# A hybrid encoder layer on one core: six passes per token half at both ends of the up phase, splits at the joint on VectorE, and the down projection's last part as a plain product

## The chip, the cores and the metric

The kernel runs on one core of one Trainium2 chip. The metric is the device time of one execution in microseconds, given as the median of several runs. One further execution was recorded by the hardware profiler; all rows of the trace come from it.

## The reference, cut to what matters

One layer of an encoder is applied with the same weights to two groups of tokens, 1024 and 256 of them, 1280 in all. The mixing part (a bidirectional gated DeltaNet and a grouped-query attention, side by side) is not touched by the change. What follows it is:

```
D_MODEL = 1024
D_FF = 4 * D_MODEL
...
    mix = jnp.concatenate([o_a, o_b], axis=-1) @ w_out
    x = x + _rmsnorm(mix, norm_mix_post)
    hm = _rmsnorm(x, norm_mlp_pre)
    f = jnp.square(jax.nn.relu(hm @ w_up)) @ w_down
    return x + _rmsnorm(f, norm_mlp_post)
```

## The kernel before

Every large product is done to nearly float32 accuracy by splitting each operand into a high half, rounded to a short format, and a low half, the rest: `split` (L77 to L80) casts on ScalarE (L79) and subtracts on VectorE or, where `leng=G` is given, on GpSimd (L80). A product is then three matmuls: high by high, low by high, high by low. G is GpSimd (POOL in the profile), V VectorE (DVE), S ScalarE (ACT), T TensorE (PE), SP the engine that issues the transfers.

**Out-projection.** A loop over ten tiles of 128 tokens (L1065 to L1091). For tile t it prepares the operands of tile t + 1 (`out_prep`), loads the rows of x (`x_tile`), issues 48 matmuls (`out_mm`), and does the two norms of tile t - 1 (`out_norm`): two large VectorE operations (L1010, L1015), each behind a chain of one-column operations. `to_M` then transposes the normed tile on TensorE (L1030) and writes four quarter blocks and three of their sums into the seven operands "mc"; two of these sums are on GpSimd. The last three tiles' `to_M` is put off into the up phase.

**Up phase.** hm @ w_up is done by Strassen-Winograd: for each 256 columns of w_up (a pass; 16 of them) and each half of the tokens (640), seven products of 12 matmuls 128x320 (`up_mm`). The seven activation operands are split once for each token half (`prep_m`, tiles mh and ml); the four sums of weight blocks are made for each pass (`up_sums`, tile us, GpSimd), and each of the seven weight operands is split for its product (`up_w`, tiles uhi and ulo). After a product VectorE adds it up from PSUM, ScalarE does relu and square, and GpSimd makes four sums s of the result (`up_post`) that the down phase needs; all seven results go to DRAM (r_d). The list PASSES orders this: the first NF = 3 passes run for token half 0 alone (single passes), since half 1 is not ready, the next 13 for both halves (double passes), and the last three for half 1 alone. Around it the loop over s, one step for each product of a pass, places by hand what else is issued: the norm and `to_M` of the last tiles in steps 0 to 4, the splits of half 1 in steps 8 to 20, alternating between GpSimd and VectorE, and from 21 steps before the end the first loads and splits of the down phase (`down_load`, with four weight sums on GpSimd; `down_r`; `down_prep`).

**Down phase.** The same algorithm over the other dimension, in eight parts of 512 rows of w_down. A part has seven steps; a step splits a row operand (fr into fhi and flo) and a weight operand (dw into dhi and dl), and `prod` does five tiles of six matmuls 128x512 and adds each from PSUM into one or two of the accumulators (ten tiles of 1024 columns).

**Last part.** The eighth part has its operands split ahead (`last_ops`, during part seven) and is done tile by tile, so that a tile is ready before the next. The two token halves of a tile need two corrections among the accumulators (`fix`, GpSimd), squares with sums on ScalarE whose unused output is a PSUM tile named junk (L1400), and the last norm (`rest`): one-column operations, a multiplication by the gain (GpSimd, L1411), the addition of x (L1423) and the write (L1425).

Instructions on one engine run in the order in which a scheduler placed them, so an instruction that waits holds all behind it.

## Time and profile before

| | |
|---|---|
| runs | 1779.65, 1782.5, 1783.88 us; median 1782.5 |
| the profiled execution's own time | 1782.71 us |
| its span | 1780.9 us |
| TensorE busy | 1634.0 us (92%), 9769 matmuls |
| VectorE busy | 1262.1 us (71%) |
| ScalarE busy | 849.0 us (48%) |
| GpSimd busy | 845.1 us (47%) |

A row of a timeline has the start in the span, the duration, engine, line and operation, then the tile written and the tiles read with their shape, and in brackets the idle time before it and what ended that. A row of a group has the line, engine, operation, tiles and count, then the busy sum in us, the mean of one in ns, and the idle time before them with those who ended it. A duration includes some pipelining: the next instruction of an engine can start before the end that is shown.

### The profile page before, as it was taken

Reading aid. Unit: us, or ns where it says so; the run is one execution under the profiler, and the core shown is the slowest. Engines: PE = TensorE matmul, PEld = TensorE weight load, DVE = VectorE, ACT = ScalarE, POOL = GpSimd, SP = SyncE. Lnnn points to the kernel's source line nnn. Section 1 sums busy time; section 2 is a strip of 40 time slices with the busy share of each in tenths; the row PEclk is TensorE's granted clock in tenths of the full one; section 3 lists DMA queues with packets and bytes.
Section 4 is the critical chain, followed back from the end, with each engine's and each line's share of the span. In section 5 each row is a group of like instructions: output and inputs, shape, how many; then the busy total and the mean of one; then the engine's idle time right before and its main releaser. Section 6 shows DMA issues by size and latency. Waiting matters only on the chain. (4 is left out here: it accounts for less than half of the span.)

```text
span 1780.9 us, 27898 instructions
## 1 busy us (share of the span) xinstructions
PE 1634.0 (92%) x9769; PEld 1395.0 (78%) x9769; DVE 1262.1 (71%) x2475; ACT 849.0 (48%) x1917; POOL 845.1 (47%) x709
## 2 busy tenths in 40 slices
PE   6999889889988999899887999999979999999984
PEld 5777777767767887578777999999978888888863
DVE  7546798996746878876667544544467878878988
ACT  5236567544336766764345454544545233333422
POOL 3212331321213344420349555445587777777855
PEclk9999999999989999999998999999989999999997
DMA  6113335455358765334323444343555444444125
GB/s 206 66 44 108 105 102 146 110 161 147 111 154 275 251 200 181 129 107 152 116 76 97 143 151 144 128 138 120 184 179 185 152 138 151 151 137 146 59 106 177
DMA packets 205516, 250.85 MB, mean 141 GB/s; under 512 B 35009, under 2 KB 159743, under 8 KB 205375
## 3 DMA queue, kind: packets, MB, share of 16 engines
q1 hardware_dynamic: 205231, 248.93, 44.1%
q8 instruction: 77, 1.26, 0.3%
q14 instruction: 64, 0.52, 0.1%
q0 software_dynamic: 144, 0.13, 0.0%
HBM read 158.57 MB, written 90.44 MB: 140 GB/s over the span
## 5 line engine op out<-in xcount | busy, mean ns | idle before, releaser
L1138 PE MATMUL pd<-mh,ulo 128*128 128x320 f32 x892 | 282.7, 317 | 19.8 <-DVE ulo L80 19.6
L1137 PE MATMUL pd<-mh,uhi 128*128 128x320 f32 x892 | 280.6, 315 | 8.4 <-ACT uhi L79 7.6
L1139 PE MATMUL pd<-ml,uhi 128*128 128x320 f32 x892 | 280.1, 314 | 0.0
L1279 DVE TENSOR_TENSOR acc<-acc,pd 128x512 f32<-128x512 f32 x380 | 238.3, 678 | 44.7 <-PE pd L1275 44.5
L1274 PE MATMUL pd<-dl,fhi 128*128 128x512 f32 x490 | 192.4, 393 | 0.0
L1273 PE MATMUL pd<-dhi,fhi 128*128 128x512 f32 x490 | 192.3, 393 | 0.0
L1275 PE MATMUL pd<-dhi,flo 128*128 128x512 f32 x490 | 191.8, 391 | 0.0
L1138 PEld LDWEIGHTS pd<-mh,ulo 128*128 128x128 f32 x892 | 172.1, 193 | 24.0 <-DVE ulo L80 24.0
L1137 PEld LDWEIGHTS pd<-mh,uhi 128*128 128x128 f32 x892 | 172.1, 193 | 10.1 <-ACT uhi L79 9.0
L369 PE MATMUL pt<-h_hi,wlo 128*128 128x512 f32 (+1 forms) x480 | 179.1, 373 | 0.0
L367 PE MATMUL pt<-h_hi,whi 128*128 128x512 f32 (+1 forms) x480 | 179.0, 373 | 0.0
L368 PE MATMUL pt<-h_lo,whi 128*128 128x512 f32 (+1 forms) x480 | 178.5, 372 | 0.0
L1139 PEld LDWEIGHTS pd<-ml,uhi 128*128 128x128 f32 x892 | 172.0, 193 | 0.0
L1255 ACT CAST fhi<-fr 128x1280 fp32r<-128x1280 f32 x49 | 62.1, 1267 | 218.2 <-PE pd L1274 120.0
L80 POOL TENSOR_TENSOR dl<-dw,dhi 128x1024 fp32r<-128x1024 f32 x49 | 130.6, 2666 | 39.6 <-ACT dhi L79 39.0
L727 POOL TENSOR_TENSOR P<-P,sm 128x512 f32<-128x512 f32 (+1 forms) x72 | 73.5, 1040 | 95.2 <-DVE sm L725 41.1
L80 DVE TENSOR_TENSOR ulo<-us,uhi 128x512 fp32r<-128x512 f32 x76 | 72.1, 951 | 52.6 <-ACT uhi L79 51.2
L1275 PEld LDWEIGHTS pd<-dhi,flo 128*128 128x128 f32 x490 | 91.9, 188 | 21.0
L1273 PEld LDWEIGHTS pd<-dhi,fhi 128*128 128x128 f32 x490 | 92.0, 188 | 20.9
L1274 PEld LDWEIGHTS pd<-dl,fhi 128*128 128x128 f32 x490 | 92.0, 188 | 20.4
L367 PEld LDWEIGHTS pt<-h_hi,whi 128*128 128x128 f32 x480 | 93.0, 194 | 13.4
L369 PEld LDWEIGHTS pt<-h_hi,wlo 128*128 128x128 f32 x480 | 92.9, 193 | 12.9
(353 smaller groups left out, 4087.7 us busy)
## 6 DMA issues: line engine op xcount, KB each, us to landing
fr<-r_d SPq DMA_DIRECT2D x49, 640.0 KB, 4.1
vis<-vis_d SPq DMA_DIRECT2D x64, 384.0 KB, 4.1
r_d<-s SPq DMA_DIRECT2D x128, 160.0 KB, 1.8
uraw<-in_w_up SPq DMA_DIRECT2D x19, 1024.0 KB, 5.3
dw<-in_w_down SPq DMA_DIRECT2D x32, 512.0 KB, 4.4
r_d<-u SPq DMA_DIRECT2D x96, 160.0 KB, 2.5
wraw<-in_w_in SPq DMA_DIRECT2D x48, 256.0 KB, 3.7
x<-in_x_prompt SPq DMA_DIRECT2D x16, 512.0 KB, 5.3
```

The costliest lines, as they stand in the source:

```text
L80: (V if leng is None else leng).tensor_tensor(lo, src, f32(hi), ALU.subtract)
L367: T.matmul(pm[:, :n], lhsT=whi, rhs=h_hi[:, k, t0:t0 + n], start=(k == 0), stop=False)
L368: T.matmul(pm[:, :n], lhsT=whi, rhs=h_lo[:, k, t0:t0 + n], start=False, stop=False)
L369: T.matmul(pm[:, :n], lhsT=wlo, rhs=h_hi[:, k, t0:t0 + n], start=False, stop=(k == KD - 1))
L727: G.tensor_tensor(x[:, :kw], x[:, :kw], sm[:, 0:1].to_broadcast([128, kw]), ALU.mult)
L1137: T.matmul(pm, lhsT=w[0][:, k], rhs=mh[b, i][:, k], start=(k == 0), stop=False)
L1138: T.matmul(pm, lhsT=w[1][:, k], rhs=mh[b, i][:, k], start=False, stop=False)
L1139: T.matmul(pm, lhsT=w[0][:, k], rhs=ml[b, i][:, k], start=False, stop=(k == 3))
L1273: T.matmul(pm, lhsT=r[0][:, k, tk], rhs=w[0][:, k], start=(k == 0), stop=False)
L1274: T.matmul(pm, lhsT=r[0][:, k, tk], rhs=w[1][:, k], start=False, stop=False)
L1275: T.matmul(pm, lhsT=r[1][:, k, tk], rhs=w[0][:, k], start=False, stop=(k == Q - 1))
L1279: V.tensor_tensor(half(t, d), half(t, d), pm, ALU.add)
```

## The change

Three things are changed together.

Single passes: NF goes from 3 to 6, so six passes run for token half 0 alone at the start of the up phase, ten for both halves, and six for half 1 alone at the end. The up phase has the same products in all.

The joint: of the seven operands of half 0, six instead of five are split before the up phase and the seventh in step 0. All these splits, those of half 1 (now in steps 10, 14, up to 34) and the two late sums of `to_M` for the last three tiles go to VectorE. In single passes `up_sums` is on VectorE as well, in double passes it stays on GpSimd. x has one buffer instead of two, and the load of tile t is issued behind the norm of tile t - 1. The norm of the last tile is put into steps 3 to 6, its `to_M` into step 7. At the end of the up phase the loads and splits of the down phase are spread over 42 steps, the weights ahead of the rows.

The last part: a plain product of 512 rows by 1024 columns, with four row blocks (one of them, a21, is now written to DRAM for the first two passes) and four weight blocks as they are loaded. Each token half of a tile and each half of its columns is one group of 12 matmuls, with one addition into its accumulator: 240 matmuls and 20 additions instead of 210 and 50. The weights' low halves are made on GpSimd during part seven, which has no sums of weights for a part eight any more. The corrections are issued a tile ahead, the squares' unused output is an SBUF tile, and the last norm is done for each token half by itself, the multiplications in two pieces of 512 columns.

The next rows show what that does to the order on three engines. TensorE in the out-projection: xt is the transposition of a normed tile, pmx the matmuls of the next tile; the piece of the difference stands near tile 7.

```order
@@ -3236,5 +3236,4 @@
 L916 MATMUL pmx<-wo_lo_9195,o_hi 128x512
 L917 MATMUL pmx<-wo_hi_9194,o_lo 128x512
-L1030 MATMUL xt<-ident,mix 128x128 x8
 L897 MATMUL otr<-ident,og 128x128 x4
 L915 MATMUL pmx<-wo_hi_9153,o_hi 128x512
@@ -3257,4 +3256,5 @@
 L917 MATMUL pmx<-wo_hi_9186,o_lo 128x512
 L915 MATMUL pmx<-wo_hi_9190,o_hi 128x512
+L1029 MATMUL xt<-ident,mix 128x128 x8
 L916 MATMUL pmx<-wo_lo_9191,o_hi 128x512
 L917 MATMUL pmx<-wo_hi_9190,o_lo 128x512
@@ -3286,7 +3286,7 @@
```

The transpositions of one tile stand further back, among the matmuls of the tile after. VectorE at the start of the up phase, before: ss and rsq belong to the last norm, mc to `to_M`, ulo to the weights' splits.

```order
L1008 TENSOR_TENSOR ss<-ss 128x1
L1040 TENSOR_TENSOR mc<-xt,mc 128x4x64
L987 TENSOR_SCALAR rsq<-ss 128x1
L80 TENSOR_TENSOR ulo<-uraw,uhi 128x512
L1041 TENSOR_TENSOR mc<-mc,xt 128x4x64
L1040 TENSOR_TENSOR mc<-xt,mc 128x4x128
L80 TENSOR_TENSOR ulo<-us,uhi 128x512
L1163 TENSOR_TENSOR u_10312<-u,pd 128x320
L80 TENSOR_TENSOR ulo<-us,uhi 128x512
```

And in the changed kernel, where us are the sums of weight blocks and ml is a split of an activation operand:

```order
L1007 TENSOR_TENSOR ss<-ss 128x1
L1039 TENSOR_TENSOR mc<-xt,mc 128x4x64
L1040 TENSOR_TENSOR mc<-mc,xt 128x4x64
L1041 TENSOR_TENSOR mc<-mc 128x4x64
L1128 TENSOR_TENSOR us<-uraw 128x512
L1042 TENSOR_TENSOR mc<-mc 128x4x64
L1129 TENSOR_TENSOR us<-us,uraw 128x512
L1130 TENSOR_TENSOR us<-uraw 128x512
L1131 TENSOR_TENSOR us<-uraw,us 128x512
L80 TENSOR_TENSOR ulo<-uraw,uhi 128x512
L80 TENSOR_TENSOR ulo<-us,uhi 128x512
L80 TENSOR_TENSOR ml<-mc,mh 128x1280
```

Sums that were on GpSimd and a split stand in VectorE's queue between the first weights' splits, and the late `to_M` stands ahead of them. VectorE in the last part, before: tile by tile, the additions of products (L1279) mixed with the results (L1423) of the tile before.

```order
L1279 TENSOR_TENSOR acc_15140<-acc_15140,pd 128x512
L1279 TENSOR_TENSOR acc_15135<-acc_15135,pd 128x512
L1423 SCALAR_TENSOR_TENSOR acc_15133<-acc_15133,rsq,x_17851 128x1024
L1279 TENSOR_TENSOR acc_15140<-acc_15140,pd 128x512
L1279 TENSOR_TENSOR acc_15135<-acc_15135,pd 128x512
L1279 TENSOR_TENSOR acc_15140<-acc_15140,pd 128x512 x2
L1279 TENSOR_TENSOR acc_15135<-acc_15135,pd 128x512 x2
L1423 SCALAR_TENSOR_TENSOR acc_15138<-acc_15138,rsq,x_17851 128x1024
L1279 TENSOR_TENSOR acc_15140<-acc_15140,pd 128x512 x2
```

And in the changed kernel, acc_15252 being token half 0 of the first tile and acc_15257 its half 1:

```order
L1456 TENSOR_TENSOR acc_15252<-acc_15252,pd 128x512 x2
L1425 TENSOR_TENSOR rsq<-ss 128x1
L1427 TENSOR_SCALAR rsq<-rsq 128x1
L1428 RECIPROCAL rsq<-rsq 128x1
L1429 SCALAR_TENSOR_TENSOR rsq<-rsq 128x1
L1430 SCALAR_TENSOR_TENSOR rsq<-rsq 128x1
L1434 SCALAR_TENSOR_TENSOR acc_15252<-acc_15252,rsq,x_17934 128x1024
L1456 TENSOR_TENSOR acc_15257<-acc_15257,pd 128x512 x2
```

The two additions of a token half are followed by its own norm and result, and these stand ahead of the next half's additions. On GpSimd all ten corrections (L1413, L1414) stand ahead of the multiplications (L1422).

The diff; lines that the old last part loses are left out, since they are shown above:

```diff
-    h_slot = {(j, 0): place(ma, 10 + i) for i, (_, j) in enumerate(UP[:5])}
-    w_slot = place(ma, 15)
+    h_slot = {}
...
     def x_tile(t):
-        x = pp.tile([128, DM], F32, tag="x", name="x", bufs=2)
+        x = pp.tile([128, DM], F32, tag="x", name="x", bufs=1)
         SP.dma_start(out=x, in_=x_rows(t))
         return x
...
-    def to_M(xn, t):
+    def to_M(xn, t, eng=G):
...
-                G.tensor_tensor(t2, b22, t1, ALU.subtract)
-                G.tensor_tensor(t4, t2, b21, ALU.subtract)
+                eng.tensor_tensor(t2, b22, t1, ALU.subtract)
+                eng.tensor_tensor(t4, t2, b21, ALU.subtract)
...
-    NF = 3
+    NF = 6
     PASSES = [*((p, (0,)) for p in range(NF)), *((p, (0, 1)) for p in range(NF, NP)), *((p, (1,)) for p in range(NF))]
...
+    NM = 6
+    h_slot |= {(j, 0): place(ma, 10 + i) for i, (_, j) in enumerate(UP[:NM])}
+    w_slot = place(ma, 10 + NM)
     prev = None
     late = []
+    x = x_tile(0)
     for t in range(NT):
         if t + 1 < NT:
             ops.append(out_prep(t + 1))
-        x = x_tile(t)
         if t:
             cur = out_mm(t, *ops[t], pp)
         if prev is not None:
             run(out_norm(t - 1, *prev))
+            x = x_tile(t)
             if t - 1 < 7:
                 to_M(prev[2], t - 1)
             else:
...
         if t == HT:
             up_raw(0)
         elif t > HT:
-            for _, j in UP[:5][(0, 1, 2, 4)[t - HT - 1]:(1, 2, 4, 5)[t - HT - 1]]:
-                prep_m(j, 0, G)
+            a, b = ((0, 1), (1, 3), (3, 4), (4, 6))[t - HT - 1]
+            for _, j in UP[a:b]:
+                prep_m(j, 0)
...
+    a21_d = dr.tile([128, Q, HW], F32, name="a21_d")
...
         a11, a12, a21, a22 = (raws[n][:, k:k + 4, f:f + 128] for f in (0, 128) for k in (0, 4))
...
-        G.tensor_tensor(s[0], a21, a22, ALU.add)
-        G.tensor_tensor(s[1], s[0], a11, ALU.subtract)
-        G.tensor_tensor(s[2], a11, a21, ALU.subtract)
-        G.tensor_tensor(s[3], a12, s[1], ALU.subtract)
+        eng = V if PASSES[n][1] != (0, 1) else G
+        eng.tensor_tensor(s[0], a21, a22, ALU.add)
+        eng.tensor_tensor(s[1], s[0], a11, ALU.subtract)
+        eng.tensor_tensor(s[2], a11, a21, ALU.subtract)
+        eng.tensor_tensor(s[3], a12, s[1], ALU.subtract)
...
+            if p < Q:
+                SP.dma_start(out=a21_d[:, p, h * SW:h * SW + SW], in_=a21)
...
     norm = out_norm(NT - 1, *prev)
     xlate = prev[2]
-    m1 = [j for _, j in UP]
+    to_M(*late[0], V)
     up_sums(0)
     ws[1] = up_w(*seq[1])
-    to_M(*late[0])
     for s, (n, i) in enumerate(seq):
         p, parts = PASSES[n]
+        if s == 1:
+            to_M(*late[1], V)
         if s + 2 < len(seq):
             ws[s + 2] = up_w(*seq[s + 2])
         w = ws.pop(s)
...
             up_post(p, i, h, up_mm(w, UP[i][1], h))
         if i == 6 and n + 2 < len(PASSES):
             up_raw(n + 2)
-        if s < 2:
-            prep_m(UP[5 + s][1], 0, G)
-        if s == 1:
-            to_M(*late[1])
-        if s in (0, 1, 2, 3):
+        if s == 0:
+            for _, j in UP[NM:]:
+                prep_m(j, 0)
+        if 2 < s < 7:
             next(norm, None)
-        elif s == 4:
-            to_M(xlate, NT - 1)
+        elif s == 7:
+            to_M(xlate, NT - 1, V)
             nstack.close()
             mr = ctx.enter_context(pool("mr"))
             h_slot |= {(j, 1): place(mr, j) for j in range(7)}
-        if 6 < s < 21 and s % 2 == 0:
-            j = m1.pop(0)
-            prep_m(j, 1, (G, None)[len(m1) % 2])
-        k = s - (len(seq) - 21)
+        if s > 9 and (s - 10) % 4 == 0 and s < 38:
+            j = UP[(s - 10) // 4][1]
+            prep_m(j, 1)
+        k = s - (len(seq) - 7 * NF)
         if k == 0:
...
-        if k in (0, 4, 7, 10):
-            down_load(0, (0, 4, 7, 10).index(k))
-        if k in (1, 2, 16, 18):
-            down_r((1, 2, 16, 18).index(k))
-        if k in (13, 17):
-            run(down_prep((13, 17).index(k)))
+        if k in (4, 12, 18, 24):
+            down_load(0, (4, 12, 18, 24).index(k))
+        k -= 7 * NF - 21
+        if k in (-3, 1, 15, 18):
+            down_r((-3, 1, 15, 18).index(k))
+        if k in (8, 13):
+            run(down_prep((8, 13).index(k)))
...
+    def last_row(x):
+        src = a21_d if x == (1, 0) else r_d[{(0, 0): 0, (0, 1): 1, (1, 1): 2}[x]][:, :Q]
+        raw = (u0, u1)[len(lrow) % 2].tile([128, Q, HW], F32, tag="uraw", name="lr", bufs=1)
+        SP.dma_start(out=raw, in_=src)
+        lrow[x] = hi, lo = [p_tile5(lslots.pop(0), (Q, HW), "lrow", F32R) for _ in range(2)]
+        split(hi, lo, raw)
+    def last_w(x):
+        raw, slot = lraw[x]
+        lwt[x] = hi, lo = [p_tile5(lslots.pop(0), (Q, 512), "lwt", F32R) for _ in range(2)]
+        split(hi, lo, raw, leng=G)
+        lslots.append(slot)
     for s in range(NS):
         n, i = divmod(s, 7)
         g = down_prep(s + 2) if s + 2 < NS else iter(())
...
                 next(g, None)
         if s + 4 < NS:
             down_r(s + 4)
...
+        if i < 4 and n < NC - 2:
             down_load(n + 1, i)
         if n == NC - 2:
...
             if i == 0:
...
+                k = slots["w", (n + 1) % 2]
+                lslots += [*k[4:], *extra]
+                src = I["w_down"][:Q * 256].rearrange("(p h r) d -> h r p d", h=2, r=128)
+                for slot, (h, d) in zip(k, ((0, 0), (1, 0), (0, 1), (1, 1))):
+                    lraw[h, d] = p_tile5(slot, (Q, 512), "lraw"), slot
+                    SP.dma_start(out=lraw[h, d][0], in_=src[h, :, :, d * 512:d * 512 + 512])
+                k = slots["w", n % 2]
+                free = [k[7], *(k[("t1", "b11", "b22", "b21", "t3", "t2", "t4").index(x[1])] for x in DN)]
             lslots.append(free[i])
...
+            for x in {1: ((0, 0),), 2: ((1, 0),), 3: (), 4: ((0, 1),), 5: ((1, 1),)}.get(i, ()):
+                last_w(x)
+            if i > 2:
+                last_row(((0, 0), (0, 1), (1, 0), (1, 1))[i - 3])
+    wpf = p_tile5(slots["fr"][0], (DM,), "wpf")
+    junk = p_tile5(slots["fr"][1], (512,), "junk", BF16)
     SP.dma_start(out=wpf, in_=I["norm_mlp_post"].partition_broadcast(128))
     def rows_of(c, h):
...
     def fix(c):
         G.tensor_tensor(half(c, 1), half(c + HT, 1), half(c, 1), ALU.subtract)
         G.tensor_tensor(half(c + HT, 0), half(c + HT, 1), half(c + HT, 0), ALU.subtract)
...
+    def rest(c, h, ss):
+        t = c + h * HT
+        last = (c, h) == (HT - 1, 1)
+        r = ac.tile([128, 4], F32, tag="rsq", name="rsq", bufs=3)
+        for d in range(2):
+            (V if last else G).tensor_tensor(half(t, d), half(t, d), wpf[:, d * 512:d * 512 + 512], ALU.mult)
+            if not last:
+                yield
+        V.tensor_tensor(r[:, 0:1], ss[:, 0:1], ss[:, 1:2], ALU.add)
+        S.activation(r[:, 1:2], r[:, 0:1], AF.Sqrt, scale=1.0 / DM, bias=eps)
+        V.tensor_scalar(r[:, 2:3], r[:, 0:1], -0.5 / DM, -0.5 * EPS, ALU.mult, ALU.add)
+        V.reciprocal(r[:, 1:2], r[:, 1:2])
+        V.scalar_tensor_tensor(r[:, 3:4], r[:, 1:2], r[:, 2:3], r[:, 1:2], ALU.mult, ALU.mult)
+        V.scalar_tensor_tensor(r[:, 3:4], r[:, 3:4], 1.5, r[:, 1:2], ALU.add, ALU.mult)
+        yield
+        for c0, n in ((0, 512), (512, 512)) if c == HT - 1 else ((0, DM),):
+            cs = slice(c0, c0 + n)
+            V.scalar_tensor_tensor(acc[t][:, cs], acc[t][:, cs], r[:, 3:4], x1s[c][:, h, cs], ALU.mult, ALU.add)
+            for ps_, t0, t1 in rows_of(c, h):
+                SP.dma_start(out=y_out(t0, t1, cs), in_=acc[t][ps_, cs])
+        if h and c + 2 < HT:
+            x1s[c + 2] = x1_tiles(c + 2)
+    x1s = {c: x1_tiles(c) for c in range(2)}
+    fix(0)
+    rests = []
+    for c in range(HT):
+        tk = slice(c * 128, c * 128 + 128)
         for h in range(2):
+            ss = ac.tile([128, 2], F32, tag="ss", name="ss", bufs=3)
             for d in range(2):
...
+                pm = p_tile()
+                for m in range(2):
+                    r, w = lrow[h, m], lwt[m, d]
+                    for k in range(Q):
+                        T.matmul(pm, lhsT=r[0][:, k, tk], rhs=w[0][:, k], start=(m == k == 0), stop=False)
+                        T.matmul(pm, lhsT=r[0][:, k, tk], rhs=w[1][:, k], start=False, stop=False)
+                        T.matmul(pm, lhsT=r[1][:, k, tk], rhs=w[0][:, k], start=False, stop=(m == k == 1))
+                t = c + h * HT
+                V.tensor_tensor(half(t, d), half(t, d), pm, ALU.add)
+                S.activation(junk, half(t, d), AF.Square, accum_out=ss[:, d:d + 1])
+                for _ in range(2):
+                    if rests and next(rests[0], "end") == "end":
+                        rests.pop(0)
+            rests.append(rest(c, h, ss))
+            if h == 0 and c + 1 < HT:
+                fix(c + 1)
     for g in rests:
         run(g)
```

More of the change, by code (lines that the diff above doesn't have):

```diff
@@ L1095, in build @@
         mc[j, 1] = p_tile5(m_slot[j, 1], name="mc")
-    for i, (_, j) in enumerate(UP[5:]):
+    for i, (_, j) in enumerate(UP[NM:]):
         h_slot[j, 0] = place(mb, i)
@@ L1331, in build @@
     acc = [ac.tile([128, DM], F32, name=f"acc{t}") for t in range(NT)]
-    lops = {}
+    lrow, lwt, lraw = {}, {}, {}
     lslots = []
-    def last_ops(j):
-        name = DN[j][1]
-        hi, lo, whi = (p_tile5(lslots.pop(0), shape, "lo", F32R) for shape in ((Q, HW), (Q, HW), (Q, 512)))
-        x = (u0, u1)[len(lops) % 2].tile([128, Q, HW], F32, tag="uraw", name="lr", bufs=1)
-        SP.dma_start(out=x, in_=r_src(NC - 1, j))
-        split(hi, lo, x)
-        lops[j] = (hi, lo), w_split(NC - 1, name, whi)
-    LORDER = (0, 2, 4, 1, 3, 5, 6)
+    def last_row(x):
[9 more added lines that the diff above has]
+        lslots.append(slot)
     for s in range(NS):
@@ L1395, in fix @@
         G.tensor_tensor(half(c + HT, 0), half(c + HT, 1), half(c + HT, 0), ALU.subtract)
-        ss = ac.tile([128, 2, 2], F32, tag="ss", name="ss", bufs=2)
-        for h in range(2):
-            for d in range(2):
-                junk = ps.tile([128, 512], F32, tag="mm", name="junk", bufs=3)
-                S.activation(junk, half(c + h * HT, d), AF.Square, accum_out=ss[:, h, d:d + 1])
-        return ss
-    def rest(c, ss):
-        r = ac.tile([128, 4, 2], F32, tag="rsq", name="rsq", bufs=2)
-        V.tensor_tensor(r[:, 0], ss[:, :, 0], ss[:, :, 1], ALU.add)
-        S.activation(r[:, 1], r[:, 0], AF.Sqrt, scale=1.0 / DM, bias=eps)
-        V.tensor_scalar(r[:, 2], r[:, 0], -0.5 / DM, -0.5 * EPS, ALU.mult, ALU.add)
-        last = c == HT - 1
-        for h in range(2):
-            (V if last and h else G).tensor_tensor(acc[c + h * HT], acc[c + h * HT], wpf, ALU.mult)
-        yield
-        V.reciprocal(r[:, 1], r[:, 1])
-        V.tensor_tensor(r[:, 3], r[:, 1], r[:, 1], ALU.mult)
-        V.tensor_tensor(r[:, 3], r[:, 3], r[:, 2], ALU.mult)
-        V.scalar_tensor_tensor(r[:, 3], r[:, 3], 1.5, r[:, 1], ALU.add, ALU.mult)
-        x1 = x1s.pop(c)
-        for h in (1, 0) if last else (0, 1):
-            yield
-            t = c + h * HT
-            for c0, n in ((0, 512), (512, 512)) if last else ((0, DM),):
-                cs = slice(c0, c0 + n)
-                V.scalar_tensor_tensor(acc[t][:, cs], acc[t][:, cs], r[:, 3, h:h + 1], x1[:, h, cs], ALU.mult, ALU.add)
-                for ps_, t0, t1 in rows_of(c, h):
-                    SP.dma_start(out=y_out(t0, t1, cs), in_=acc[t][ps_, cs])
-        if c + 2 < HT:
@@ L1427, in rest @@
             x1s[c + 2] = x1_tiles(c + 2)
     x1s = {c: x1_tiles(c) for c in range(2)}
+    fix(0)
     rests = []
-    for cs in ((0, 1), (2,), (3,), (4,)):
-        for k, j in enumerate(LORDER):
-            for c in cs:
-                prod(*lops[j], c, DN[j][2])
-            if k > 0 and rests and next(rests[0], "end") == "end":
-                rests.pop(0)
-        for g in rests:
-            run(g)
-        rests = [rest(c, ss) for c, ss in [(c, fix(c)) for c in cs]]
+    for c in range(HT):
+        tk = slice(c * 128, c * 128 + 128)
+        for h in range(2):
+            ss = ac.tile([128, 2], F32, tag="ss", name="ss", bufs=3)
+            for d in range(2):
+                pm = p_tile()
[14 more added lines that the diff above has]
+                fix(c + 1)
```

11 lines of the change are left out of this document (removed).

## The prediction

> **What bounds the kernel now.** I read the page first, then a table of windows over the last layer part, then groups, waits and timelines inside each window.
>
> ```profile
> span 1780.9 us, 27898 instructions
> ```
>
> The profiled execution took 1782.71 us by its own time, 1.8 us of it outside the span, and the runs have a median of 1782.5; the sum below is made against 1782.7. The change touches only what follows 790 us. The windows there (length, then the busy time of each engine, granted clock, DMA share) are the joint from the out-projection to the up phase, its first 66 us, the double passes of the up phase, its end, the down phase, its last part, and the tail:
>
> ```profile
> core 0: us, PE busy (x) PEld busy (x) DVE busy (x) ACT busy (x) POOL busy (x), PEclk, DMA share, GB/s
> 914.00:1021.00 107.00, 87.98 (x525) 84.75 (x523) 74.64 (x94) 55.81 (x106) 84.44 (x56) 0.89 0.35 116
> 914.00:980.00 66.00, 46.98 (x246) 43.75 (x244) 52.30 (x58) 34.68 (x63) 59.36 (x34) 0.82 0.29 93
> 1021.00:1282.00 261.00, 261.00 (x1783) 261.00 (x1782) 129.05 (x224) 131.36 (x267) 135.33 (x128) 1.00 0.41 138
> 1282.00:1357.00 75.00, 64.52 (x402) 61.60 (x402) 52.29 (x61) 38.05 (x72) 57.52 (x38) 0.93 0.59 197
> 1357.00:1695.00 338.00, 338.00 (x1471) 275.64 (x1471) 278.54 (x380) 115.51 (x107) 265.41 (x101) 1.00 0.43 139
> 1695.00:1760.00 65.00, 53.13 (x212) 41.39 (x211) 56.95 (x76) 15.58 (x39) 43.42 (x20) 0.95 0.41 130
> 1760.00:1781.00 21.00, 0.66 (x3) 0.19 (x2) 13.59 (x23) 3.08 (x9) 8.23 (x4) 0.60 0.35 136
> ```
>
> In the two long windows PE never idles at clock 1.00; nothing done there can help. They give the rates: 261/1783 = 0.146 us for an up matmul (12.3 us for the 84 of a single pass) and 338/1471 = 0.230 us for a down matmul. Against these the other windows lose time. The joint holds 525 matmuls, 19 of them transposes or of the out-projection by my count, so 506 × 0.146 = 74.1 of 107 us: 32.9 lost. The end of the up phase has 402 × 0.146 = 58.9 of 75: 16.1 lost. The last part has 210 × 0.230 = 48.3 of 65: 16.7 lost, and 21 of tail follow it. Who is late at the joint is in the groups of its first 66 us (busy, mean ns, idle time before and its releaser):
>
> ```profile
> L1138 PE MATMUL pd<-mh,ulo 128*128 128x320 f32 x72 | 26.7, 371 | 14.6 <-DVE ulo L80 14.6
> L80 POOL TENSOR_TENSOR ml<-mc,mh 128x1280 fp32r<-128x1280 f32 x6 | 18.9, 3156 | 0.1
> ```
>
> PE waits for the low halves of the weights that DVE makes, while POOL, busy 59 of 66 us, works on the splits of the activations.
>
> **The change, part by part.**
>
> A, out-projection. Here POOL's three splits hold DVE's norm, and PE waits for that norm's result. The rows are POOL, DVE twice, PE, then the x tile's normal durations (min/median/max) and its load:
>
> ```profile
> 864.82 9.73 POOL L80 TENSOR_TENSOR ml<-mc,mh 128x1280 fp32r<-128x1280 f32 x3
> 864.79 4.05 DVE L1010 SCALAR_TENSOR_TENSOR x<-mix,rsq,x 128x1024 f32<-128x1024 f32 x1
> 871.85 3.79 DVE L1015 SCALAR_TENSOR_TENSOR mix<-x,rsq,wpm 128x1024 f32<-128x1024 f32 x1
> 875.78 0.45 PE L1030 MATMUL xt<-ident,mix 128*128 128x128 f32 x1 [6.78 <-DVE mix L1015]
> L1010 DVE SCALAR_TENSOR_TENSOR x<-mix,rsq,x x10: 1283/1286/4052, 801.3 to 927.3; 128x1024 f32<-128x1024 f32 x10
> DMA to landing us min/median/max: 2.6/2.6/6.1
> ```
>
> Two operations of 1.29 became 4.05 and 3.79, and PE stood 6.78 us. With the splits on DVE POOL is idle there, and the transposes now stand some 18 matmuls later in PE's queue. DVE does pay for the splits, but between tiles where it has slack. I take −6 (bounds −8, with the clock lost behind the gap, to 0, if the splits on DVE delay the norm as long). One x buffer instead of two costs nothing: its load lands in 2.6 us, and the tiles come 126/9 = 14 us apart; without that cover it would be 2.6 per tile. The load now waits on SP for the norm before it, and behind it stand only out_prep's loads, wanted a tile later.
>
> B, joint. DVE is the engine to count. Its operations with two SBUF inputs cost by what POOL does meanwhile. First alone (start to next start), then the PSUM adds, then means in the three windows 1021:1282, 914:1021 and 1282:1357:
>
> ```profile
> 941.00 0.68 DVE L80 TENSOR_TENSOR ulo<-uraw,uhi 128x512 fp32r<-128x512 f32 x1
> 941.61 0.47 DVE L1178 TENSOR_TENSOR u<-u,pd 128x320 f32<-128x320 f32 x1
> 963.92 0.48 DVE L1173 TENSOR_TENSOR u<-u,pd 128x320 f32<-128x320 f32 x1
> 964.32 0.47 DVE L1174 TENSOR_TENSOR u<-u,pd 128x320 f32<-128x320 f32 x1
> L80 DVE TENSOR_TENSOR ulo<-us,uhi 128x512 fp32r<-128x512 f32 x41 | 30.0, 733 | 35.1 <-ACT uhi L79 34.0
> L80 DVE TENSOR_TENSOR ulo<-uraw,uhi 128x512 fp32r<-128x512 f32 x33 | 29.5, 893 | 3.0 <-ACT uhi L79 1.8
> L80 DVE TENSOR_TENSOR ulo<-us,uhi 128x512 fp32r<-128x512 f32 x20 | 22.7, 1141 | 8.4 <-ACT uhi L79 8.1
> L80 DVE TENSOR_TENSOR ulo<-uraw,uhi 128x512 fp32r<-128x512 f32 x13 | 14.6, 1120 | 0.4 <-ACT uhi L79 0.3
> L80 DVE TENSOR_TENSOR ulo<-us,uhi 128x512 fp32r<-128x512 f32 x15 | 19.4, 1296 | 9.1 <-ACT uhi L79 9.0
> L80 DVE TENSOR_TENSOR ulo<-uraw,uhi 128x512 fp32r<-128x512 f32 x10 | 13.9, 1390 | 6.9 <-ACT uhi L79 6.8
> 987.75 0.88 POOL L1191 TENSOR_TENSOR s<-s,u 128x320 f32<-128x320 f32 x1
> ```
>
> Call the cost of one such 512-wide operation L. Alone it is 0.60 (941.00 to 941.61); the mean duration, less 0.07 of overlap with the next, is 0.73 where POOL is busy 135.33/261 = 0.52 of the time, 1.06 at 84.44/107 = 0.79 and 1.26 at 57.52/75 = 0.77. A PSUM add takes 0.40 from start to start and never more. In the new joint six single passes run, and POOL has only their s operations, 4 × 0.88 of 12.3 us, a share of 0.29: L = 0.60 + 0.13 × 0.29/0.52 = 0.67; I take 0.70, since DVE is denser there. DVE's list to the end of the sixth pass: 43 low halves and 24 sums are 67 L; 8 activation splits of 1280 columns, 2.5 times as wide, 20 L; 41 PSUM adds 16.4; 12 operations of to_M at 0.60 or less, 7.2; the last norm, two of 1.29 and small ones, 3.3. That is 87 L + 26.9 = 87.8. DVE idled 66 − 52.30 = 13.7 us in the joint's first window; I keep 10 for start and hand-overs: 97.8 against 107, **−9**. Bounds: L = 0.60 without idling, 79.1 and −28; L = 1.06 with 13.7 idle, 132.8 and +26.
>
> A row speaks against this: ulo beside POOL's work is up to twice as long, though POOL's own operation is shorter. The Trainium skill, "SBUF — State Buffer", section "Who interferes with whom", says that a DVE instruction with two SBUF inputs contends with a GpSimd instruction that reads SBUF; for operations that hold both ports it has the loser block fully. The trace agrees that PSUM adds (one SBUF input) never stretch. By a full block all 24 s operations, 21.1 us, would add to 79.1 + 10: 110, B = +3, and a total of 1757.
>
> C, end of the up phase. The waits there:
>
> ```profile
> ACT fhi L1255 <- DMA fr<-r_d: 13.6, 3, 8.9
> PE pd L1137 <- ACT uhi L79: 5.2, 1, 5.2
> PE pd L1138 <- DVE ulo L80: 5.0, 6, 2.4
> ```
>
> ACT, in order, stands at a cast whose rows have not landed, and the casts of the weights (uhi) queue behind it; PE pays 5.2. DVE pays for POOL's burst, 5.0. The new schedule spreads down_load and the row loads over 42 steps instead of 21, and the sums leave POOL. DVE gets them: per pass 11 L + 7 × 0.40, over six passes 66 L + 16.8, against 73.8 of PE. POOL's share there I estimate at 40/74 = 0.54 (24 s operations 21 us, the four sums of down weights and some five splits 19), so L = 0.75: 66.3, below PE. So of the 10.2 of waits I take back **−8**; the second fhi cast still stands among uhi casts. Bounds −13 (most of 16.1) and +16 (L = 1.26, 100 − 73.8 − 10).
>
> D, last part and tail. Groups of the last part, then single rows:
>
> ```profile
> L1279 DVE TENSOR_TENSOR acc<-acc,pd 128x512 f32<-128x512 f32 x51 | 32.1, 675 | 0.8 <-PE pd L1275 0.7
> L1273 PE MATMUL pd<-lo 128*128 128x512 f32 x70 | 29.4, 422 | 11.9 <-ACT junk L1400 6.1 <-DVE acc L1279 5.8
> L1400 ACT ACTIVATE junk<-acc 128x512 f32<-128x512 f32 x20 | 11.9, 596 | 47.7 <-DVE acc L1279 19.0 <-POOL acc L1394 16.5 <-DVE rsq L1414 6.7
> 1722.48 1.27 POOL L1395 TENSOR_TENSOR acc<-acc 128x512 f32<-128x512 f32 x1
> 1726.13 2.33 DVE L1408 TENSOR_SCALAR rsq<-rsq 128x2 f32<-128x2 f32 x1
> 1770.69 0.92 DVE L1406 TENSOR_TENSOR rsq<-ss 128x2 f32<-128x2 f32 x1 [2.52 <-ACT junk L1400]
> 1771.53 1.21 DVE L1411 TENSOR_TENSOR acc<-acc,wpf 128x1024 f32<-128x1024 f32 x1
> 1773.56 2.74 DVE L1423 SCALAR_TENSOR_TENSOR acc<-acc,rsq,x 128x512 f32<-128x512 f32 x4
> ```
>
> The span has 1780.9 − 1695 = 85.9 us from here. The plain product has 240 matmuls, 55.1 us, 6.8 more than before, but 20 adds instead of 50, and the squares no longer write a PSUM buffer (6.1 us of PE's waits). POOL's ten corrections, 12.7 us, begin some 4.5 before the part, as soon as the last step's adds are in; its two multiplications of the first tile follow, and the first result stands at about 12. DVE's queue then ties one tile to the next: two adds 1.3, Square 0.8 with its sum, the norm's small operations 2.9 − 1.2 = 1.7 (1770.69 to 1773.56 without the multiplication), the result 1.3, hand-overs 0.6: c = 5.7 a tile, beside 5.5 for PE's 24 matmuls. After eight such cycles the last tile has adds and Square 1.4, 2.9, and the 7.3 from 1773.56 to the end less two of four halves, 5.9. So 12 + 8c + 10.2 = 67.8, −18; PE alone would give 55.1 + 10.2 = 65.3, −20. A small operation took 2.33 us beside POOL's multiplications, so I take **−15**; at c = 7 it is −8. The rows and weights of this part are loaded and split in the part before it, where PE was never short, and down_load's four sums are gone from POOL there. The four writes to a21_d, as large as those to r_d, find the DMA engines at 0.41 of their time in the double passes' window and at 0.59 at most; I cost them at nothing.
>
> Sum: −6 − 9 − 8 − 15 = −38, 1782.7 − 38 = 1744.7, so 1745. A measurement of this kernel can tell about 0.2%, 3.6 us, from no change.
>
> **Rivals.**
> 1. Moved work buys nothing: DVE and POOL together carry no more than before, and B = C = 0 (L = 0.82 at the joint would do it). For it: L rises to 1.06 and 1.26 where both are busy. Against: POOL's part at the joint shrinks from 84 us to 21. Time 1782.7 − 6 − 15 = 1761.7. The Trainium skill, "Perfetto Trace Analysis", section "Optimizing Scalar/DVE Operations", warns that moving operations between these two might not help because they share a read port; no run here has tried it.
> 2. The last part is chained: the multiplications hold DVE's small operations by some 1.7 us a tile, c = 7.4, 22.2 + 59.2 = 81.4, D = −5. For it: the 2.33 above. Time 1754.7. Both at once: 1771.7.
> 3. Slower: DVE becomes the bound of all twelve single passes. Joint and end together are then (87 L + 36.9 − 107) + (66 L − 67) with A and D −21: zero at L = 1.03. At 1.26, which the end shows today, it is +35, 1817. Against: POOL's share must stay near 0.77, with half its work gone.
> 4. All falls to PE: −8 − 28 − 13 − 20 = −69, 1714.
>
> **How the numbers follow.** Chances: forecast 0.60; rival 1 0.16; rival 2 0.10; rival 3 0.08, of which 0.03 near its zero; rival 4 0.06. So faster 0.92, same 0.03, slower 0.05. The low end takes the four distances to the lower bounds (2, 19, 5, 5) as independent: root of squares 20, 1724. The high end is rivals 1 and 2 together, 1772. Left out are rivals 3 and 4, 0.14.
>
> **What would show it.** Right: no wait of PE for L1014's result near 875; ulo means near 0.8 us in the first six passes, the joint at about 98 us to the end of the sixth; no stretch over 5 us at the end of the up phase for uhi; 68 to 71 us from the last part's first matmul to the end. Wrong: ulo means above 1.1 in the first passes, with PE waiting on them; a DVE idle time before L1434 that POOL's L1422 ends in every tile; or PE waits inside the double passes or the down phase, which I count as untouched.

## The result, and the profile after

The changed kernel takes 1739.37 us, the median of four runs (1737.97 to 1741.06), against 1781.08 for the kernel before on the same chip (1777.37 to 1783.88): a ratio of 0.9767, with a 95% interval of 0.9745 to 0.979. The profiled execution took 1741.06 us. Its span and the windows that answer to those of before are these (length, busy time of each engine, granted clock):

```profile
span 1739.3 us, 27944 instructions
```

```profile
core 0: us, PE busy (x) PEld busy (x) DVE busy (x) ACT busy (x) POOL busy (x), PEclk, DMA share, GB/s
904.70:998.10 93.40, 82.88 (x531) 78.33 (x530) 89.56 (x141) 60.49 (x115) 33.60 (x23) 0.98 0.45 147
998.10:1240.00 241.90, 241.90 (x1653) 241.90 (x1652) 126.69 (x210) 119.35 (x243) 129.10 (x118) 1.00 0.44 146
1240.00:1332.50 92.50, 82.57 (x534) 80.03 (x534) 78.02 (x109) 54.95 (x109) 43.32 (x34) 0.96 0.60 201
1332.50:1671.80 339.30, 338.30 (x1472) 275.81 (x1472) 276.24 (x380) 112.11 (x104) 260.77 (x101) 1.00 0.44 139
1671.80:1727.50 55.70, 55.70 (x242) 45.02 (x240) 37.88 (x69) 15.66 (x45) 31.34 (x26) 1.00 0.43 136
1727.50:1739.30 11.80, 0.25 (x2) 0.00 (x0) 7.16 (x16) 1.78 (x6) 0.92 (x1) 0.66 0.23 89
```

The joint is 93.4 us for the work that took 108 before, and VectorE, busy 89.56 of it, is now its fullest engine. The last part has no idle TensorE at all, and 11.8 us of tail instead of 21. The end of the up phase lost about as much time as before: its 534 matmuls at 0.146 us are 78 of 92.5 us.

The stages are compared between fixed points: the first and last matmul of the out-projection, the last of the up phase, the last of part seven of the down phase, and the end of the span. The rows with first and last start, of the kernel before:

```profile
L917 PE MATMUL pmx<-wo_hi,o_lo x160: 387/389/628, 774.1 to 913.0; 128*128 128x512 f32 x160
L1139 PE MATMUL pd<-ml,uhi x892: 303/309/468, 918.5 to 1357.1; 128*128 128x320 f32 x179
L1275 PE MATMUL pd<-dhi,flo x490: 387/390/398, 1357.7 to 1695.4; 128*128 128x512 f32 x164
```

and of the changed one:

```profile
L917 PE MATMUL pmx<-wo_hi,o_lo x160: 387/389/474, 772.5 to 904.6; 128*128 128x512 f32 x160
L1147 PE MATMUL pd<-ml,uhi x892: 305/309/468, 912.9 to 1332.5; 128*128 128x320 f32 x179
L1285 PE MATMUL pd<-dhi,flo x490: 387/390/398, 1333.1 to 1671.8; 128*128 128x512 f32 x164
```

From the same rows of every kernel that was run comes this table (us; the stages are read from one profiled execution each, and each ratio is taken against runs of the kernel before on the same chip):

| kernel | out-projection | up phase | parts 1 to 7 | last part and tail | measured median | ratio to before, interval |
|---|---|---|---|---|---|---|
| before | 138.9 | 444.1 | 338.3 | 85.5 | 1781 | 1 |
| changed | 132.1 | 427.9 | 339.3 | 67.5 | 1739.4 | 0.9767, 0.9745 to 0.979 |
| d_alone | 139.5 | 444.3 | 338.9 | 67.7 | 1761.6 | 0.9893, 0.9874 to 0.9912 |
| d_old | 131.9 | 427.8 | 339.2 | 86.7 | 1758.2 | 0.9872, 0.9857 to 0.9888 |
| a_alone | 131.3 | 444.5 | 338.8 | 85.9 | 1769.5 | 0.9945, 0.9928 to 0.9963 |
| a_ml_pool | 141.5 | 427.8 | 339.3 | 67.5 | 1752.3 | 0.9844, 0.9821 to 0.9867 |
| b_three | 131.7 | 427.7 | 338.7 | 67.7 | 1736.4 | 0.9752, 0.9737 to 0.9767 |
| b_sums_pool | 131.7 | 435.6 | 338.9 | 67.8 | 1747.4 | 0.9809, 0.9779 to 0.9838 |
| b_back | 131.8 | 441.2 | 339.2 | 67.6 | 1754.2 | 0.9846, 0.9816 to 0.9875 |
| b_no_sums | 131.8 | 419.8 | 338.9 | 67.5 | 1730.2 | 0.9725, 0.9704 to 0.9746 |
| c_fhi_pool | 132.0 | 428.2 | 339.3 | 67.5 | 1737.8 | 0.9752, 0.972 to 0.9784 |
| c_both_pool | 132.0 | 427.1 | 339.1 | 67.5 | 1738.4 | 0.9765, 0.9747 to 0.9784 |
| c_no_sums | 132.1 | 427.4 | 339.5 | 67.5 | 1737.8 | 0.9769, 0.9749 to 0.9789 |
| d_first_dve | 132.3 | 427.6 | 339.1 | 66.1 | 1739.8 | 0.9766, 0.9739 to 0.9794 |

The change gains 6.8 us in the out-projection, 16.2 in the up phase and 18.0 at the end, and loses 1.0 in parts one to seven (one wait of TensorE for an addition by VectorE, near 1345 us); 1.6 of the spans' 41.6 lie ahead of the first point, where nothing was changed.

### The profile page after: what moved, and what is told of

It reads as the page before. It is cut to its first block, busy times and chain, and to the rows that moved or that the text cites. A ratio compares the mean times of both kernels' runs of the same rounds, so it can differ in the third digit from the quotient of the medians.

```text
span 1739.3 us, 27944 instructions
## 1 busy us (share of the span) xinstructions
PE 1626.4 (94%) x9799; PEld 1387.8 (80%) x9799; DVE 1267.9 (73%) x2549; ACT 854.6 (49%) x1937; POOL 735.8 (42%) x658
## 3 DMA queue, kind: packets, MB, share of 16 engines
q8 instruction: 77, 1.26, 0.3%
## 5 line engine op out<-in xcount | busy, mean ns | idle before, releaser
L1145 PE MATMUL pd<-mh,uhi 128*128 128x320 f32 x892 | 276.6, 311 | 5.5 <-ACT uhi L79 5.5
L1289 DVE TENSOR_TENSOR acc<-acc,pd 128x512 f32<-128x512 f32 x330 | 206.7, 678 | 44.1 <-PE pd L1285 44.1
L1190 POOL TENSOR_TENSOR s<-u,u 128x320 f32<-128x320 f32 x32 | 34.3, 1071 | 207.6 <-ACT u L1155 140.7
L80 DVE TENSOR_TENSOR ulo<-us,uhi 128x512 fp32r<-128x512 f32 x88 | 76.3, 869 | 43.4 <-ACT uhi L79 42.5
```

The lines of the kernel that those rows point to most:

```text
L80: (V if leng is None else leng).tensor_tensor(lo, src, f32(hi), ALU.subtract)
L1145: T.matmul(pm, lhsT=w[0][:, k], rhs=mh[b, i][:, k], start=(k == 0), stop=False)
L1289: V.tensor_tensor(half(t, d), half(t, d), pm, ALU.add)
```

## The experiments

**The parts add up.** d_alone is the kernel before with the new last part and the writes to a21_d; d_old is the changed kernel with the old functions `last_ops`, `fix` and `rest` and the old loop in their place.

> The kernel before with the new last part alone (plain product, a21 written to DRAM, its own last norm for each token half). Theory: the parts of the change add up, and the last part is worth what the two traces show from its first matmul to the end, 85.5 - 67.5 = 18 us: 1763. Rival: part of these 18 us hangs on the new schedule ahead of it, and the part alone brings 10 us or less: 1771 or more.

> The changed kernel with the old last part (seven products, squares into PSUM). Theory: 18 us are given back, 1739 + 18 = 1757, all of them behind the first matmul of the last part. Rival: the two halves of the change need each other, and the sum of the two losses is not 42 us.

The last part and tail read 67.7 us in the one and 86.7 in the other, and the other stages of each are those of the kernel it came from. By the medians, against 1780.9 for the kernel before on that chip, 19.3 us were won by the last part alone and 22.7 by the rest, 42.0 together, which is the whole. Both rivals fell.

**The splits of the out-projection.** a_alone changes one line of the kernel before, a_ml_pool the same line of the changed one the other way:

```diff
-                prep_m(j, 0, G)
+                prep_m(j, 0)
```

> The kernel before with one thing changed: the five activation splits of the out-projection on VectorE. Theory: TensorE's wait of 6.8 us for a transposition goes, the out-projection is 7 us shorter, and nothing else moves: 1781 - 7 = 1774. Rival: GpSimd, freed early, and VectorE, loaded, only shift the wait into the joint, which is 5 us or more longer: 1779 or more.

> The changed kernel with the six activation splits of the out-projection back on GpSimd. Theory: they hold VectorE's norm as before, TensorE waits some 7 us for a transposition, 1739 + 7 = 1746. Rival 1: the transpositions now stand 18 matmuls (18 x 0.227 = 4 us) later, so only 7 - 4 = 3 us come back, 1742. Rival 2: VectorE is relieved of six splits and nothing is lost, 1739.

In a_alone the out-projection falls by 7.6 us and the up phase moves by 0.4, as the theory has it. (Its median is 4.5 us below 1774, but in its profiled execution the out-projection also begins 8.7 us earlier, ahead of what differs.) With this line alone the one transposition that had waited already stands 19 matmuls further back, among those of the next tile, so that move belongs to the engine of the splits, not to the rest of the change. In a_ml_pool it stands at its old place again, right behind the tile's last matmul: the place that rival 1 takes for granted is gone, and the run does not test it. There 9.4 us come back, more than any of the numbers. The rows of its GpSimd and VectorE (start, duration), then its TensorE:

```profile
864.45 12.69 POOL L80 TENSOR_TENSOR ml<-mc,mh 128x1280 fp32r<-128x1280 f32 x4
```

```profile
864.42 4.05 DVE L1009 SCALAR_TENSOR_TENSOR x<-mix,rsq,x 128x1024 f32<-128x1024 f32 x1
...
871.32 2.88 DVE L990 SCALAR_TENSOR_TENSOR rsq<-rsq 128x1 f32<-128x1 f32 x1
874.23 3.98 DVE L1014 SCALAR_TENSOR_TENSOR mix<-x,rsq,wpm 128x1024 f32<-128x1024 f32 x1
```

```profile
878.36 0.88 PE L1029 MATMUL xt<-ident,mix 128*128 128x128 f32 x3 [9.73 <-DVE mix L1014]
```

Four splits now follow one another on GpSimd, one more than before, and three of VectorE's operations, one of them on a single column, last nearly as long as one of GpSimd's (12.69/4 = 3.2 us) or longer. TensorE stands 9.73 us.

Was the norm early again with the splits on VectorE? The changed kernel's TensorE, where the four transpositions otr follow the tile's last matmul, and its VectorE:

```profile
867.41 0.60 PE L897 MATMUL otr<-ident,og 128*128 128x128 f32 x4
...
873.52 1.07 PE L1029 MATMUL xt<-ident,mix 128*128 128x128 f32 x8 [1.16 <-DVE rsq L988]
```

```profile
865.42 1.49 DVE L80 TENSOR_TENSOR ml<-mc,mh 128x1280 fp32r<-128x1280 f32 x1
866.83 1.28 DVE L1009 SCALAR_TENSOR_TENSOR x<-mix,rsq,x 128x1024 f32<-128x1024 f32 x1
...
872.08 1.29 DVE L1014 SCALAR_TENSOR_TENSOR mix<-x,rsq,wpm 128x1024 f32<-128x1024 f32 x1
```

It was not. The norm's operations have their normal length, but its result stands at 873.4 us, 6.0 us after TensorE was done with the tile, since five splits of 1.5 us stand among the operations ahead of it. A tile earlier, without splits, the result is there 1.1 us before that point (854.1 against 855.2). In a_alone it comes 6.0 us after it too, in the kernel before 6.6 (875.6 against 869.0). What saves TensorE is the place of the transposition: 19 matmuls and otr fill 5.0 us, and 1.2 us of waiting are left. With the transposition at its old place TensorE would have stood about 6 us, an estimate from these rows. Why the order moves with the engine of the splits is not shown.

**Six passes or VectorE.** b_three sets NF back to 3, with the splits of half 1 on VectorE in steps 8 to 20 and the old steps for the down phase's loads; b_back keeps NF = 6 and puts all that the up phase moved back on GpSimd; b_sums_pool moves only the sums of weight blocks back:

```diff
-    NF = 6
+    NF = 3
```

```diff
-        eng = V if PASSES[n][1] != (0, 1) else G
+        eng = G
...
-    to_M(*late[0], V)
+    to_M(*late[0])
...
-                prep_m(j, 0)
+                prep_m(j, 0, G)
...
-            prep_m(j, 1)
+            prep_m(j, 1, (G, None)[(s - 10) // 4 % 2])
```

> The changed kernel with three single passes at each end instead of six (half 1 split on VectorE in steps 8, 10 up to 20, the down phase's first loads at the old steps). Theory (VectorE's list bounds the joint): three single passes hold 34 operations of 512 columns with two SBUF inputs and 20 such units of splits, 54 x 0.75 + 8 + 10 = 59 us, then the double passes are bound by TensorE, 21 products x 1.76 = 37: 96 us against the 93.5 of six passes, so 2 to 3 us slower, 1742. Rival: it is the six passes that give the gain, since TensorE has products of half 0 while half 1 is being split: the joint returns to 103 or more, 1749 or more.

> The changed kernel with all that was moved to VectorE in the up phase back on GpSimd (sums of weight blocks, the seventh split, the splits of half 1 in turn with VectorE, the late sums of to_M); the six splits of the out-projection stay on VectorE, and the six single passes stay. Theory: the moves to VectorE, not the six passes, carry the gain of the joint, so most of its 14.5 us come back: 1750 or more. Rival: with six passes the same work on GpSimd has 93 us instead of 65 and is no longer late, so either half of the change would do: 1743 or less.

> The changed kernel with the sums of weight blocks on GpSimd in all passes, the single ones too; all else as changed. Theory (VectorE's list bounds the joint): 24 operations of 0.68 us leave VectorE there, 16 us, but GpSimd's share of the time rises from 0.36 to about (33.6 + 31)/93 = 0.69, and by the table of the prediction the other 67 units cost about 0.25 us more, 17 us: no change, 1739, within 4. Rival: GpSimd is again late with the sums at each pass's start, and TensorE waits for them: the joint returns to 100 us or more, 1746 or more.

b_three has the same up phase as the changed kernel, 427.7 us: with the moves made, the six passes give nothing, and neither its rival's loss nor the theory's 2 to 3 us is there. (Its median is 3 us lower, but its out-projection begins at 768.9 instead of 772.5, ahead of all that differs.) b_back loses 13.3 of the 16.2 us, so the moves to VectorE carry the gain and the rival falls; the six passes alone are worth at most the other 2.9. b_sums_pool loses 7.7 us where the theory had none, and its time, 1747.4, is the rival's. Its joint is not: by the last addition of the sixth pass it is 3.3 us late (97.6 us after the out-projection instead of 94.3), within the theory's 4; the other 4.4 are lost after it, where the theory did not look. The costs in the joint are as the theory had them. First b_sums_pool's groups on VectorE, then those of the changed kernel:

```profile
L80 DVE TENSOR_TENSOR ulo<-us,uhi 128x512 fp32r<-128x512 f32 x25 | 27.1, 1087 | 3.5 <-ACT uhi L79 3.5
L80 DVE TENSOR_TENSOR ulo<-uraw,uhi 128x512 fp32r<-128x512 f32 x19 | 19.8, 1045 | 0.2 <-ACT uhi L79 0.2
```

```profile
L80 DVE TENSOR_TENSOR ulo<-us,uhi 128x512 fp32r<-128x512 f32 x24 | 20.9, 877 | 0.3 <-ACT uhi L79 0.3
L80 DVE TENSOR_TENSOR ulo<-uraw,uhi 128x512 fp32r<-128x512 f32 x19 | 15.7, 826 | 0.2
L80 DVE TENSOR_TENSOR ml<-mc,mh 128x1280 fp32r<-128x1280 f32 x8 | 12.8, 1600 | 0.0
...
L1129 DVE TENSOR_TENSOR us<-us,uraw 128x512 f32<-128x512 f32 x6 | 4.1, 679 | 0.0
```

With the sums on GpSimd the low halves take 1.07 us, with the sums on VectorE 0.85, and three of VectorE's own four sums 0.68 (the fourth, L1128, 0.79).

**What bounds the joint now.** b_no_sums leaves the sums out in the first six passes and uses raw blocks in their place:

```diff
+        if n < NF:
+            ua[n] = [a11, a12, a22, a21, a11, a12, a22]
+            return
```

> The changed kernel without the sums of weight blocks in the first six passes: raw blocks are taken as operands in their place, so those passes compute another product than the reference's. Theory (VectorE's list bounds the joint: it was busy 89.6 of 93.4 us): 24 operations, 16 us, leave it, and the joint falls to 79 to 83 us, TensorE's 74 and some start: 1726 to 1729. Rival: the joint is set by the chain of cast, low half and product for each weight, not by VectorE's load, and falls by 4 us or less: 1735 or more.

The up phase falls by 8.1 us, between the two numbers: 16 us of VectorE buy half of that. TensorE's waits there, in the changed kernel and then without the sums:

```profile
PE pd L1146 <- DVE ulo L80: 5.4, 9, 1.2
PE pd L1145 <- ACT uhi L79: 3.0, 4, 1.7
```

```profile
PE pd L1149 <- DVE ulo L80: 3.2, 4, 1.5
PE pd L1148 <- ACT uhi L79: 1.1, 3, 0.4
```

VectorE's list does bound the joint, but taking 16 us from it shortens the joint by 8 only. What bounds the rest was not taken apart; TensorE's products alone are 74 us.

**The end of the up phase.** Three kernels tried to free it. c_fhi_pool casts the first two row operands on GpSimd, c_both_pool makes their low halves there too, and c_no_sums leaves out the sums in the last six passes (the lines of b_no_sums with n >= NP). The copy's line below is that of both first kernels, the two conditions are c_both_pool's alone.

```diff
-        S.copy(hi, fr[s])
-        if i % 2:
+        (S.copy if s > 1 else G.tensor_copy)(hi, fr[s])
+        if i % 2 or s == 0:
...
-        if i % 2 == 0:
+        if i % 2 == 0 and s:
```

> The changed kernel with the first two row operands of the down phase cast on GpSimd instead of ScalarE. Theory: what the end of the up phase still loses begins where ScalarE stands 5.1 us at the second of these casts, whose rows have not landed, with the weights' casts queued behind it; TensorE idles about 5 us there and then runs some 8 us at a granted clock of 0.5 to 0.7. Off ScalarE that goes: 1739 - 7 = 1732. Rival: VectorE's split of the same rows waits as well and holds the low halves of the weights, or GpSimd's longer cast holds the sums s: 1737 to 1740.

> The changed kernel with both the cast and the low half of the first two row operands of the down phase on GpSimd, so that neither ScalarE nor VectorE waits for rows that have not landed. Theory: the run before, with the casts alone moved, lost on VectorE (5.4 us behind the low half of the first row operand) what it won on ScalarE; with both gone the end of the up phase is 4 to 6 us shorter, 1734. Rival: VectorE's own work or GpSimd's port bounds the end, and it stays at 92 us, 1738 to 1740.

> The changed kernel without the sums of weight blocks in the last six passes (raw blocks are taken in their place, so those passes compute another product than the reference's). Theory: the end of the up phase fell short because the sums that VectorE was given there, 24 operations of some 0.8 us, use up what the quieter GpSimd wins, and TensorE waits for the low halves of weights behind them: without them the end is 6 to 10 us shorter, 1730 to 1733. Rival: something else holds VectorE and ScalarE there (the rows that land late, the transfers), and it is 2 us or less shorter, 1737 or more.

None of them freed it: the up phase is 428.2, 427.1 and 427.4 us against 427.9. The stall is there in the changed kernel. ScalarE's cast waits for its rows, and in windows of 4 us TensorE's busy time and then its granted clock fall:

```profile
1261.13 1.26 ACT L1265 CAST fhi<-fr 128x1280 fp32r<-128x1280 f32 x1 [5.09 <-DMA fr<-r_d]
```

```profile
1260.00:1264.00 4.00, 1.26 (x7) 0.77 (x5) 1.21 (x2) 2.84 (x5) 1.53 (x1) 0.97 1.02 387
1264.00:1268.00 4.00, 2.04 (x8) 2.04 (x9) 3.45 (x5) 1.92 (x5) 1.97 (x2) 0.50 0.46 150
1268.00:1272.00 4.00, 4.00 (x21) 4.00 (x21) 2.50 (x3) 1.89 (x5) 3.62 (x4) 0.68 0.43 149
```

But each remedy meets another wait. With the casts on GpSimd, VectorE waits for one of them; with both halves on GpSimd only ScalarE waits for rows, 2.9 us for a later operand's, and TensorE still waits 8.5 us for low halves; without the sums ScalarE's wait is longer. The rows of waits of c_fhi_pool, c_both_pool and c_no_sums:

```profile
DVE flo L1271 <- POOL fhi L1265: 5.4, 1, 5.4
```

```profile
PE pd L1146 <- DVE ulo L80: 8.5, 11, 2.1
```

```profile
ACT fhi L1268 <- DMA fr<-r_d: 9.3, 2, 7.2
```

TensorE's waits at the end of the up phase, for low halves and casts together, are 9.9 us in the changed kernel, 10.3, 9.1 and 9.6 in these three, and 10.2 in the kernel before: they change their name and keep their sum. That two causes lie over each other there, the late rows and VectorE's load, and that taking away both would free the end, is what these rows suggest; it was not tried.

**The last part's chain.** d_first_dve puts one tile's two multiplications on VectorE:

```diff
-            (V if last else G).tensor_tensor(
+            (V if last or t == 0 else G).tensor_tensor(
```

> The changed kernel with the last norm's multiplication of the first token half of the first tile on VectorE. Theory: the last part is a chain on VectorE, 12 us to the first result, which waits for the ten corrections and two multiplications of GpSimd, and 5.62 us for each token half after; TensorE ends 4 to 5 us ahead of the last addition. With the first result some 4 us earlier the part ends 3 to 4 us earlier, 1735.5. Rival: the chain waits for GpSimd's next multiplications, and the part stays at 67.5 us, 1739.

The last part shortens by 1.4 us, not 3 to 4. The results of the first three token halves on VectorE in the changed kernel, with the two additions behind the first, and the three results in d_first_dve, whose last part begins 2.4 us earlier (1669.4 instead of 1671.8):

```profile
1683.79 1.28 DVE L1434 SCALAR_TENSOR_TENSOR acc<-acc,rsq,x 128x1024 f32<-128x1024 f32 x1 [1.26 <-POOL acc L1422]
1684.99 1.28 DVE L1456 TENSOR_TENSOR acc<-acc,pd 128x512 f32<-128x512 f32 x2
...
1689.41 1.28 DVE L1434 SCALAR_TENSOR_TENSOR acc<-acc,rsq,x 128x1024 f32<-128x1024 f32 x1
...
1695.04 1.28 DVE L1434 SCALAR_TENSOR_TENSOR acc<-acc,rsq,x 128x1024 f32<-128x1024 f32 x1
```

```profile
1681.27 1.28 DVE L1434 SCALAR_TENSOR_TENSOR acc<-acc,rsq,x 128x1024 f32<-128x1024 f32 x1
...
1685.64 1.28 DVE L1434 SCALAR_TENSOR_TENSOR acc<-acc,rsq,x 128x1024 f32<-128x1024 f32 x1
...
1691.27 1.28 DVE L1434 SCALAR_TENSOR_TENSOR acc<-acc,rsq,x 128x1024 f32<-128x1024 f32 x1
```

The chain is there, 5.6 us from result to result. The first result stands at 12 us in both. In the changed kernel it waits 1.26 us for GpSimd's multiplication, as its row says; in d_first_dve the two multiplications take 1.6 and 1.5 us of VectorE's time, beside GpSimd's corrections, and the gain is spent. Only from the second result on is the chain earlier, by 1.4 us.

No kernel that was run beats the changed one by a margin that these intervals allow, except those that leave work out.

## Why the prediction was right, and where it was not

The time was forecast at 1745 and the gain at 38; measured were 1739.4 and, by the medians, 41.7. That the sum came so near is in part luck: B and D gave 8.5 us more than forecast and C 6.3 less. B and D have the right mechanism; A's size came by the second of its two reasons; C's mechanism failed.

- **A, out-projection, −6.** Measured −6.8, and −7.6 in a_alone. That GpSimd's splits held the norm is as the row of 4.05 us said. What failed is the sentence that VectorE pays for them between tiles, where it has slack: there they delay the norm's result to 6.0 us after the tile, hardly less than the 6.6 of before, the case that the bound of 0 names. The 6 us were won because the transposition stands 19 matmuls later, the reason given beside it, which the bound of 0 left out.
- **B, joint, −9.** Measured −14.5 (93.5 us for 108.0). VectorE's list was forecast at 87.8, and VectorE is busy for 89.56. What failed is the 10 us kept for start and hand-overs: VectorE idles 93.4 − 89.6 = 3.8, and 2 of these lie at the start. For L 0.70 was taken; the low halves took (20.9 + 15.7)/43 − 0.07 = 0.78, the sums and the splits less than 0.70 a unit, so that the list came out nearly as forecast. The forecast counted a joint of six passes; it did not see that three give the same.
- **C, end of the up phase, −8.** This step failed: measured −1.7 (336.1 to 334.4 us from the point where 42 products are done). Two of its sentences were wrong. The new steps of the loads did not place the casts of the rows: the first two stand behind 111 and 118 casts of weights in both kernels' order, though their steps differ. With six single passes 35 casts of weights follow the second instead of 14, so it comes earlier before the end (71 us instead of 34), but its rows are late still: ScalarE stands 5.1 us at it, where it stood 8.9. And the 10.2 us of waits were added as if they were separate: TensorE waits 7.5 us for low halves and 2.4 for casts there after the change, 9.9 in all. The sign that the prediction named, no stretch over 5 us for uhi, came true (the longest is 2.1) while the time did not: the wait went over to the low halves. The moved sums did help, for b_sums_pool loses 4.4 us after the sixth pass and waits 5.5 us for casts at the end; what the change gives back beside them is not shown by any run.
- **D, last part and tail, −15.** Measured −18.0; the sum's 67.8 us are 67.5, with c = 5.62 for 5.7 and the first result at 12.0 for 12. The 3 us kept back for small operations held by GpSimd were not needed. They are held, but two of them for each token half by some 0.5 us (one in the first by 1.1), where before it was up to 2.2, as the second row shows beside its neighbour of one column:

```profile
1688.24 0.16 DVE L1428 RECIPROCAL rsq<-rsq 128x1 f32<-128x1 f32 x1 [0.17 <-ACT rsq L1426]
1688.44 0.69 DVE L1429 SCALAR_TENSOR_TENSOR rsq<-rsq 128x1 f32<-128x1 f32 x1
```

The multiplications now come in pieces of 1.27 us; that this is why the holds are shorter was not tried by itself.

Rival 1 (moved work buys nothing) fell with b_back: the moves are worth 13.3 us. GpSimd's share, the reason given against it, fell as said, and the low halves with it (1.22 us at a share of 0.88 in b_back, 0.78 at 0.36). The total of 1757 put all 21.1 us of GpSimd's sums s on VectorE; that is too dear. By an estimate, GpSimd's work added 43 × 0.17 = 7 us to the joint's 43 low halves (0.85 against 0.68 for VectorE's own sums). The block itself is there, but it goes both ways. The same section of the Trainium skill, "SBUF — State Buffer", "Who interferes with whom", says that issue order decides who blocks. The trace agrees, as neighbours from the joint of the changed kernel show, first VectorE, then GpSimd:

```profile
946.53 1.48 DVE L80 TENSOR_TENSOR ml<-mc,mh 128x1280 fp32r<-128x1280 f32 x1
947.98 1.32 DVE L80 TENSOR_TENSOR ulo<-us,uhi 128x512 fp32r<-128x512 f32 x1
949.23 0.47 DVE L1171 TENSOR_TENSOR u<-u,pd 128x320 f32<-128x320 f32 x1
```

```profile
947.16 1.60 POOL L1190 TENSOR_TENSOR s<-u,u 128x320 f32<-128x320 f32 x1 [13.70 <-ACT u L1155]
948.71 1.33 POOL L1192 TENSOR_TENSOR s<-u,u 128x320 f32<-128x320 f32 x1
```

GpSimd's sum begins inside VectorE's split, takes 1.60 us instead of 0.88 and ends 0.75 us after it; the low half begins inside that sum, takes 1.32 instead of 0.68 and ends 0.5 us after it; the next sum begins inside the low half and takes 1.33. The split, which was first, has its normal 1.48, and the addition from PSUM its 0.47. Over the joint GpSimd's 20 sums take 29.7 us instead of 20 × 0.88 = 17.6: some 12 us of the collisions fall on GpSimd, which is busy for only 33.6 of 93.4 us and has the time.

Rival 2 has the right chain and a wrong price, 7.4 for 5.62. Rivals 3 and 4 did not come.

## What to carry to other kernels

Count an engine's list of operations in the stage that is late, each at the price it has beside its neighbour's load, and do not add idle time to a list that never lacks work. Waits of one stage that name different engines are not to be added up as gains: free one, and the next may end at the same time. Where a scheduler places instructions, compare their order before giving a moved line of code any effect, or before putting a gain down to the line: in the out-projection the result stayed late, and the instruction that waits for it had moved.
